# Shorter fixed ends of the first layer's MLP, and second-attention queries made turned in the first layer

## The chip, the cores and the metric

The kernel runs on one core of one Trainium2 chip. The metric is the device time of one execution in microseconds (us). A core has a matrix engine (PE in the profile; its weight loads stand apart as PEld), a vector engine (DVE), a scalar engine (ACT), a third elementwise engine (POOL), a queue engine that starts transfers (SP), and 16 DMA engines. PE multiplies a stationary operand of 128x128 with a moving one (at most 512 columns here) and adds into a PSUM bank (tiles of 128x512 fp32). The kernel uses two rings of four such banks, named `acc` and `misc`.

## The reference

Two layers over 256 tokens of width 1024, in fp32. Each layer is

```python
h = rms_norm(x, attn_norm[l])
p = h @ w_in[l]      # c_q, c_kv, k_rope | mq, mk, mv | rq, rk, rv, rg | three gates
o_mla  = causal attention, 8 heads; q and k, v come from normed c_q (256) and c_kv (128)
o_moba = causal attention, 8 heads of 64: softmax(rope(mq) rope(mk)^T) mv   # one block of 256 holds all tokens
o_ret  = retention, 4 heads, then group norm and silu(rg)
merged = sum over the three of sigmoid(gate) * (o @ w_branch)
x = x + merged @ w_out[l]
h = rms_norm(x, mlp_norm[l])
x = x + square(relu(h @ w_mlp_up[l])) @ w_mlp_down[l]        # 1024 -> 4096 -> 1024
```

and a last `rms_norm` ends it. "Second attention" is `o_moba`; its queries are `mq`, its keys `mk`, its values `mv`. The names `b0` and `c0` stand for the product that holds c_q, c_kv and k_rope (416 columns).

## The kernel before

**Products in three parts.** Every fp32 operand is split into a high part of type fp32r and a low part, the remainder, of the same type. ACT writes the high part (`whi`, L202, for a weight tile; L238 for an activation), DVE the low part (`wlo`, L204; L239). A product is then high by high, high by low and low by high (`three`, L222 to L225). A weight tile is 128x1024: 512 KB, one transfer from SP (L187), one split on ACT and one on DVE. Seven raw tiles and six split ones are held at a time. `load_w` fetches tiles in the order of `weight_plan`, one tile ahead of the one in use. What runs ahead on ACT and DVE is decided by the tile scheduler, which orders the instructions of each engine when the kernel is built, by a simulated clock; `tc.manual_schedule` and `tc.keep_in_program_order` fix the order of what stands in them.

**Two ways round.** `project` keeps tokens on the output's partitions: activations are stationary, weights move. `project_turned` (L371) makes the transposed product: 128 weight columns are stationary, and the high and low halves of the activations move side by side (512 columns, L380), then the low weights with the high half (256 columns, L382). The two halves of the result are joined by an ACT copy (L386) and a DVE add (L387), "the join", and the bank is free after that.

**The program of a layer** is a list `prog` of units (one weight tile or a few), with steps hung on units by `at(slot(unit, j), step)`. Layer 0 begins with eight `start` units, one for each 128 rows of `x`: each multiplies b0 (two `misc` banks) and mq (two `acc` banks, tokens on partitions). When the last is done, `moba_done` copies mq out on ACT (L682) and applies the rotary embedding on DVE; `c_norms` (L648) copies b0 out on ACT (L657), squares it (L660, L661), and norms it; later `moba_turn` (L854) transposes mq on PE, four 128x128 transposes for each half (L860). Layer 1 makes mq by `project_turned` and applies the rotary embedding by `moba_rope` on POOL (`rope_turned` with four small transfers from SP and three POOL operations for each half). In both layers mk is turned: four units `mk 0` to `mk 3` follow, each in one `acc` bank.

**The MLP** walks 32 tiles `f` of the width 4096. `up` makes two of them (L1075: 512 columns; L1077: 256), `squared_relu` splits the result, and `down` (L1091) adds each tile into four quarters of the output (two token halves by two column halves, one `acc` bank each). The last `ENDS = 4` tiles are kept back: their `down` runs quarter by quarter, 12 matmuls each. The last tile (`WHOLE = 1`) is made by `project_t`, with the three parts of 256 columns in one half bank. At the end of layer 0 each quarter, once complete, is copied by ACT (`copied`, L1148), transposed by PE (`turned`, L1154), added to `x` by DVE (L1156), and split for the next layer's norm (`take_part`: four L238 on ACT, four L239 on DVE). The next layer's b0 begins with token half 0 and goes on with half 1; `before(i)` runs the last quarter's `turned(3)` ahead of b0's third unit. The squares of `x` (L271, L274) are summed by POOL (L275) and give the norm's statistics (L295).

Of the kernel before, what the change touches and what calls it, by code (L numbers as in the profile page):

```python
# [18 lines left out]
L = 2  # L19
# [3 lines left out]
ENDS = 4  # L23
# [27 lines left out]
def weight_plan():  # L51
# [14 lines left out]
    for l in range(L):  # L66
# [36 lines left out]
        for f in range(0, NF + 2, 2):  # L103
            for i in (f, f + 1) if f < NF else ():
                block((l, "up", i), "w_mlp_up", KD, span(P * i, P), KD)
            for i in (f - 2, f - 1) if 2 <= f <= NF - ENDS else ():
                plan.append(((l, "down", i, 0), "w_mlp_down", (i, 1), range(D)))
        for i in range(NF - ENDS, NF):
            plan.append(((l, "down", i, 0), "w_mlp_down", (i, 1), range(D)))
# [12 lines left out]
K_COS_MB = K_SIN_MLA + NT * 16  # L122
K_SIN_MB = K_COS_MB + NT * 8

K_TURNED_MLA = K_SIN_MB + NT * 8
# [13 lines left out]
def trunk(ctx: ExitStack, tc: tile.TileContext, gx, wts, consts, gfin, gn, xtok, out):  # L139
# [96 lines left out]
    def split(src, hi, lo, scale):  # L236

        nc.scalar.activation(hi, src, AF.Copy, scale=scale)  # L238
        nc.vector.scalar_tensor_tensor(lo, src, scale, hi.bitcast(F32), op0=ALU.mult, op1=ALU.subtract)  # L239

    def split_plain(src, hi, lo):
        nc.scalar.activation(hi, src, AF.Copy)
        nc.vector.tensor_sub(lo, src, hi.bitcast(F32))
# [4 lines left out]
    class Normed:  # L248
# [28 lines left out]
        def take_part(self, t, half):  # L277

            sl = slice(P * t, P * t + P)
            for n in range(4 * half, 4 * half + 4):  # L280
                hi, lo = self.k(n)
                split(chunk(n)[:, sl], hi[:, sl], lo[:, sl], gain(self.g0 + n))
# [87 lines left out]

    def project_turned(l, key, xn, done):  # L371


        pair = []

        def unit(n):
# [6 lines left out]
            if n % 2 == 0:  # L383
                pair.append(w2k("qkraw"))
            second = sb.tile([P, S], F32, name="second", tag="relu", bufs=3)
            nc.scalar.copy(second, acc[:, S : 2 * S])  # L386
            nc.vector.tensor_add(halves(pair[-1])[:, n % 2, :], acc[:, 0:S], second)  # L387
            if n % 2:
                done(n // 2, pair[-1])
# [251 lines left out]
    def layer(l, xn, before):  # L641
# [6 lines left out]
        def c_norms():  # L648
            accs = b0
            if l:  # L650
                for n in range(KD):
                    xn.square(n)
                xn.stats()
            for t in range(NT):
                ct = w2k("c0")
                c0.append(ct)
                nc.scalar.activation(ct[:, :416], accs[t][:, :416], AF.Copy, scale=xn.col[t])  # L657
                m = small("ssc")
                junk = sb.tile([P, S], F32, name="junk", tag="xsq", bufs=2)
                nc.scalar.activation(junk, ct[:, 0:MLA_QR], AF.Square, accum_out=m[:, 0:1])  # L660
                nc.scalar.activation(junk[:, :MLA_KVR], ct[:, MLA_QR : MLA_QR + MLA_KVR], AF.Square, accum_out=m[:, 1:2])  # L661
                nc.vector.tensor_scalar(m[:, 2:3], m[:, 0:1], 1.0 / MLA_QR, EPS, op0=ALU.mult, op1=ALU.add)
                nc.vector.tensor_scalar(m[:, 3:4], m[:, 1:2], 1.0 / MLA_KVR, EPS, op0=ALU.mult, op1=ALU.add)
                nc.gpsimd.tensor_tensor(m[:, 4:6], m[:, 2:4], neghalf[:, 0:2], op=ALU.pow)
                nc.vector.tensor_scalar(ct[:, 0:MLA_QR], ct[:, 0:MLA_QR], m[:, 4:5], None, op0=ALU.mult)
                kv = ct[:, MLA_QR : MLA_QR + MLA_KVR]
                nc.vector.tensor_scalar(kv, kv, m[:, 5:6], None, op0=ALU.mult)
                kr = ct[:, 384:416].rearrange("p (h two n) -> p h two n", h=1, two=2)
                rope(kr, K_COS_MLA, K_SIN_MLA, t, 16, 1)
                for i in range(2):  # L670
                    dst = krx[t][:, 64 * (1 - i) : 64 * (1 - i) + 64].rearrange("p (two n) -> p two n", two=2)
                    nc.vector.tensor_copy(dst[:, :, 16 * i : 16 * i + 16], kr[:, 0, :, :])

# [4 lines left out]
        def moba_done(key):  # L678
            def done(accs):
                dst = mqkv[key] = [w2k(key) for _ in range(NT)]  # L680
                for t in range(NT):
                    nc.scalar.activation(dst[t], accs[t], AF.Copy, scale=xn.col[t])  # L682
                    if key == "mq":
                        xv = dst[t].rearrange("p (h two r) -> p h two r", h=MB_H, two=2)[:, :, :, 0:8]
                        rope(xv, K_COS_MB, K_SIN_MB, t, 8, MB_H)
# [3 lines left out]
        def start(k, mq):  # L689

            if k == 0:
                b0.extend(misc_tile("b0") for _ in range(NT))
                mq.extend(acc_tile() for _ in range(NT))
            before(k)
            ah, al = xn.k(k)
            if k == 0:

                blocks = [(mq, slice(0, 256), load_w(l, "mq", 0), 0, True), (mq, slice(256, 512), load_w(l, "mq", 1), 0, False)]
                blocks.append((b0, slice(0, 416), load_w(l, "b0", 0), 0, True))
            else:  # L700
                w = load_w(l, "b0mq", k)
                blocks = [(b0, slice(0, 416), w, 0, False), (mq, slice(0, 512), w, 416, False)]

            for part in ("high", "low"):
                for accs, cs, w, c, begins in blocks:
                    ws = slice(c, c + cs.stop - cs.start)
                    for t in range(NT):
                        o, sl = accs[t][:, cs], slice(P * t, P * t + P)
                        if part == "high":
                            nc.tensor.matmul(o, ah[:, sl], w[0][:, 0, ws], start=begins, stop=False)  # L710
                            nc.tensor.matmul(o, al[:, sl], w[0][:, 0, ws], start=False, stop=False)  # L711
                        else:
                            nc.tensor.matmul(o, ah[:, sl], w[1][:, 0, ws], start=False, stop=k == KD - 1)  # L713
            if k == KD - 1:
                moba_done("mq")(mq)
# [14 lines left out]
        if l:  # L730
            project_turned(l, "mq", xn, moba_pair("mq"))
            at(slot("mq", 1), c_norms)
            at(slot("mq", 2), xn.stats_row)
        else:
# [3 lines left out]
            at(slot("start", KD - 2), lambda: xn.stats_rows(xrows))  # L738
            at(slot("start", KD - 1), c_norms)
# [6 lines left out]
        def c_turn():  # L746
# [5 lines left out]
            for k in range(3):  # L752
                pt = pts[k // 2][:, (k % 2) * S : (k % 2) * S + S]
                for t in range(NT):
                    nc.tensor.transpose(pt[:, P * t : P * t + P], c0[t][:, P * k : P * k + P], ident)
# [98 lines left out]
        def moba_turn(i):  # L854

            pt = misc_tile("pq")
            for a in range(2):
                for t in range(NT):
                    k = 2 * i + a
                    nc.tensor.transpose(  # L860
                        pt[:, (2 * a + t) * P : (2 * a + t + 1) * P], mqkv["mq"][t][:, P * k : P * k + P], ident
                    )
            o = sb.tile([P, 2 * S], F32, name="qkT", bufs=4)
            nc.scalar.copy(o, pt)
            qkT["mq"][i] = halves(o)

# [137 lines left out]
        at(slot("rg", 0), lambda: in_a_row(ret_scores, moba_last))  # L1004
# [55 lines left out]
        def up(fs, between=None):  # L1060
# [4 lines left out]
            if fs[0] >= NF - WHOLE:  # L1065
# [14 lines left out]
        def squared_relu(f, u):  # L1080
            s = sb.tile([P, S], F32, name="relu", bufs=3)
            if f < NF - WHOLE:
                nc.scalar.copy(s, u[:, S : 2 * S])
                nc.vector.tensor_add(s, u[:, 0:S], s)
            nc.vector.scalar_tensor_tensor(s, s if f < NF - WHOLE else u[:, 0:S], 0.0, xm.row, op0=ALU.max, op1=ALU.mult)  # L1085
            nc.scalar.activation(s, s, AF.Square)  # L1086
            both = sb.tile([P, 2, S], F32R, name="sq", tag="w2k", bufs=W2K)
            split_plain(s, both[:, 0, :], both[:, 1, :])
# [26 lines left out]
        h2 = {}  # L1115
# [192 lines left out]
```

## Time and profile before

| | |
|---|---|
| median of 3 runs | 836.45 us (836.05 to 836.94) |
| the profiled execution, its own time | 836.87 us |
| its span in the trace | 835.1 us |
| busy: PE, PEld, DVE, ACT, POOL | 827.2, 702.9, 585.2, 482.1, 92.5 us |
| HBM read, written | 151.00 MB, 1.05 MB |

A row of a timeline gives start, length, engine, line, operation, tiles and shape; "x4" joins four in a row, and the bracket tells how long the engine had idled before it and what released it. Matmuls overlap in the pipeline (a 512-column one lasts 0.39 us, and the next starts 0.23 us later), so costs of PE are taken from start to start, or from the chain of work that ended last, which lists each piece by what it added.

### The profile page before, as it was taken

The numbers are of one execution on the slowest core, as the hardware profiler recorded it, in microseconds if no ns is written. First come the engines' busy times: TensorE is split into PE (matmuls) and PEld (weight loads), VectorE is DVE, ScalarE is ACT, GpSimd is POOL, SyncE is SP. The second block draws the span as 40 slices with busy tenths as digits, with TensorE's granted clock in tenths as the row PEclk, the third lists the DMA queues.
The fourth block names the chain that finished last, engine by engine and source line by source line (L and its number), as shares of the span: only waits on it lengthen the run. The fifth ranks groups of instructions, "written<-read, shape, count | busy, mean of one in ns | idle before, by whom it ended". The sixth has DMA issues, their size and how long they took to land.

```text
span 835.1 us, 12150 instructions
## 1 busy us (share of the span) xinstructions
PE 827.2 (99%) x4374; PEld 702.9 (84%) x4374; DVE 585.2 (70%) x1057; ACT 482.1 (58%) x858; POOL 92.5 (11%) x82
## 2 busy tenths in 40 slices
PE   9999999999999999999999999999999999999997
PEld 7888878888888888888889888888888888888886
DVE  6878567595787666666599876766868776556663
ACT  7766665445556555555676575664545555555552
POOL 0221000040030000000038111002201200000000
PEclk9999999999999999999999999999999999999999
DMA  9956644646456566565466657545565656666611
GB/s 349 362 177 212 228 141 146 195 133 219 140 187 225 183 199 186 193 193 167 131 227 194 204 178 236 157 142 188 156 199 161 219 171 192 198 196 187 197 53 50
DMA packets 45708, 155.98 MB, mean 187 GB/s; under 512 B 5712, under 2 KB 6736, under 8 KB 45392
## 3 DMA queue, kind: packets, MB, share of 16 engines
q1 hardware_dynamic: 45072, 154.54, 58.4%
q8 instruction: 34, 0.56, 0.3%
q10 hardware_dynamic: 576, 0.67, 0.2%
q14 instruction: 26, 0.21, 0.1%
HBM read 151.00 MB, written 1.05 MB: 182 GB/s over the span
## 4 chain that ended last, share of the span: by engine, by line
PE 98%; DVE 1%; ACT 0%; issue 0%; DVEq 0%
PE acc L223 18%; PE acc L225 18%; PE acc L224 18%; PE pup L1075 14%; PE pup L1077 7%; PE acc L1025 5%; PE acc L380 4%; PE acc L382 2%; PE ps_pt L483 1%; PE ps_s L835 1%; PE po L510 1%; PE ps_s L449 1%; DVE wlo L204 1%; PE acc L710 1%; PE acc L711 1%; PE acc L713 0%
## 5 line engine op out<-in xcount | busy, mean ns | idle before, releaser
L204 DVE TENSOR_TENSOR wlo<-raw,whi 128x1024 fp32r<-128x1024 f32 (+4 forms) x287 | 346.7, 1216 | 181.5 <-ACT whi L202 128.1
L202 ACT ACTIVATE whi<-raw 128x1024 fp32r<-128x1024 f32 (+4 forms) x287 | 292.0, 1023 | 188.4 <-PE acc L225 105.6
L1075 PE MATMUL pup<-xs,whi 128*128 128x512 f32 x496 | 121.5, 390 | 0.0
L225 PE MATMUL acc<-whi,xs 128*128 128x512 f32 (+1 forms) x304 | 119.3, 393 | 0.4 <-DVE xs L239 0.4
L223 PE MATMUL acc<-whi,xs 128*128 128x512 f32 (+1 forms) x304 | 119.6, 395 | 0.0
L224 PE MATMUL acc<-wlo,xs 128*128 128x512 f32 (+1 forms) x304 | 118.9, 391 | 0.0
L1075 PEld LDWEIGHTS pup<-xs,whi 128*128 128x128 f32 x496 | 91.9, 188 | 18.3
L223 PE MATMUL acc<-whi,sq 128*128 128x512 f32 x256 | 100.1, 391 | 0.0
L224 PE MATMUL acc<-wlo,sq 128*128 128x512 f32 x256 | 99.9, 390 | 0.0
L225 PE MATMUL acc<-whi,sq 128*128 128x512 f32 x256 | 98.8, 389 | 0.0
L1077 PE MATMUL pup<-xs,wlo 128*128 128x256 f32 x496 | 68.8, 283 | 0.0
L1077 PEld LDWEIGHTS pup<-xs,wlo 128*128 128x128 f32 x496 | 65.7, 191 | 3.1
L225 PEld LDWEIGHTS acc<-whi,xs 128*128 128x128 f32 x304 | 57.1, 188 | 12.3 <-DVE xs L239 0.7
L223 PEld LDWEIGHTS acc<-whi,xs 128*128 128x128 f32 x304 | 57.1, 188 | 11.7 <-issue 0.8
L224 PEld LDWEIGHTS acc<-wlo,xs 128*128 128x128 f32 x304 | 57.2, 188 | 10.5
L1086 ACT ACTIVATE relu<-relu 128x256 f32<-128x256 f32 x64 | 25.5, 408 | 54.4 <-DVE relu L1085 54.4
L225 PEld LDWEIGHTS acc<-whi,sq 128*128 128x128 f32 x256 | 48.1, 188 | 10.2
L223 PEld LDWEIGHTS acc<-whi,sq 128*128 128x128 f32 x256 | 48.2, 188 | 9.2
L224 PEld LDWEIGHTS acc<-wlo,sq 128*128 128x128 f32 x256 | 48.2, 188 | 8.9
L275 POOL TENSOR_TENSOR sqsum<-sqsum,xsq 128x256 f32<-128x256 f32 x21 | 23.3, 1111 | 290.8 <-issue 172.4
L472 ACT ACTIVATE prob<-prob,smx 128x128 f32<-128x128 f32 x64 | 28.4, 445 | 24.9 <-DVE smx L469 24.9
L380 PE MATMUL acc<-xs,whi 128*128 128x512 f32 x160 | 41.3, 395 | 0.7 <-DVE qkraw L387 0.7
(239 smaller groups left out, 1147.6 us busy)
## 6 DMA issues: line engine op xcount, KB each, us to landing
raw<-wts SPq DMA_DIRECT2D x264, 512.0 KB, 4.2
raw<-wts SPq DMA_DIRECT2D x6, 464.0 KB, 7.8
qkoth<-qkraw SPq DMA_DIRECT2D x40, 64.0 KB, 4.3
dec<-consts SPq DMA_DIRECT2D x2, 1024.0 KB, 5.0
raw<-wts SPq DMA_DIRECT2D x4, 416.0 KB, 3.2
xrow<-xtok SPq DMA_DIRECT2D x4, 256.0 KB, 8.0
gn<-gn SPq DMA_DIRECT2D x2, 512.0 KB, 5.5
raw<-wts SPq DMA_DIRECT2D x3, 256.0 KB, 4.1
```

The lines of the kernel that those rows point to most:

```text
L202: nc.scalar.activation(hi[:, cs], raw[:, cs], AF.Copy)
L204: nc.vector.tensor_sub(lo[:, cs], raw[:, cs], hi[:, cs].bitcast(F32))
L223: nc.tensor.matmul(o, ah, bh, start=start, stop=False)
L224: nc.tensor.matmul(o, ah, bl, start=False, stop=False)
L225: nc.tensor.matmul(o, al, bh, start=False, stop=stop)
L275: (nc.gpsimd if n < self.on_pool else nc.vector).tensor_add(self.sum, self.sum, sq)
L380: nc.tensor.matmul(acc, wh[:, k, :], xn.both(k), start=k == 0, stop=False)
L472: nc.scalar.activation(p[:, a:b], p[:, a:b], AF.Exp, bias=m[:, 2 + i : 3 + i], scale=scale, accum_out=m[:, 4 + i : 5 + i])
L1025: nc.tensor.matmul(o, a, b, start=half == 0 and i == 0, stop=4 * half + n == KD and i == len(jobs) - 1)
L1075: nc.tensor.matmul(u, w, xm.both(k), start=k == 0, stop=False)
L1077: nc.tensor.matmul(u[:, 0:S], w, xm.k(k)[0], start=False, stop=k == KD - 1)
L1086: nc.scalar.activation(s, s, AF.Square)
```

## The change

- `ENDS` and `WHOLE` become lists by layer. Layer 0 keeps back two tiles instead of four, and its last tile is made in a pair like the others; layer 1 stays as it was. In layer 0 the four quarters end in plain order, six matmuls each.
- At the end of layer 0, four of the next layer's weight tiles (b0 0 to 3) are fetched ahead of the quarters (`have`). `behind` names instructions that a tile's splits are scheduled behind: b0 2 and 3 behind the split of the last MLP tile, mq 0 behind the last quarter's splits. The first quarter's copy and add keep their place in the program.
- Layer 0's mq is made turned inside the `start` units, in four `acc` banks, and joined in the last unit; the weights of mk 1 and mk 2 are split behind the joins. `moba_turn`, the old rotary embedding of mq and its tables in `consts` go; `moba_rope` runs for mq in layer 0 too, at `gmla1`.
- b0 is copied and squared without the norm's factor (`c_copies`), which is applied afterwards (`c_norms`); in layer 1 the squares of `x` move from mq 1 to b0's last unit, with two of the eight sums on DVE, and the copies to mq 0.
- The retention scores move from slot `rg` 0 to `rg` 1 in both layers.

```diff
-ENDS = 4
+ENDS, WHOLE = [2] * (L - 1) + [4], [0] * (L - 1) + [1]
...
     def load_w(*key):
         ahead = 0 if key[:2] in ((0, "b0"), (0, "mq"), (0, "b0mq")) else AHEAD
-        while order and len(loaded) < ahead + 1:
+        have(min(ahead + 1, len(loaded) + len(order)))
+        return loaded.pop(key)
+    behind = {}
+    def have(n):
+        while len(loaded) < n:
             first = order.pop(0)
-            loaded[first] = fetch(first)
-        return loaded.pop(key)
+            with ExitStack() as pinned:
+                for ins in behind.get(first, ()):
+                    pinned.enter_context(tc.issue_after(ins.ins))
+                loaded[first] = fetch(first)
...
+    def joins(done):
+        pair = []
+        def join(n, acc):
+            if n % 2 == 0:
+                pair.append(w2k("qkraw"))
+            second = sb.tile([P, S], F32, name="second", tag="relu", bufs=3)
+            both = nc.scalar.copy(second, acc[:, S : 2 * S]), nc.vector.tensor_add(
+                halves(pair[-1])[:, n % 2, :], acc[:, 0:S], second
+            )
+            if n % 2:
+                done(n // 2, pair[-1])
+            return both
+        return join
...
-        def c_norms():
-            accs = b0
-            if l:
-                for n in range(KD):
-                    xn.square(n)
-                xn.stats()
+        def c_copies():
             for t in range(NT):
                 ct = w2k("c0")
-                nc.scalar.activation(ct[:, :416], accs[t][:, :416], AF.Copy, scale=xn.col[t])
...
+                nc.scalar.activation(ct[:, :416], b0[t][:, :416], AF.Copy)
...
-                mq.extend(acc_tile() for _ in range(NT))
+                mq.extend(acc_tile() for _ in range(4))
...
+            def turned_part(part, ns):
+                for n in ns:
+                    if part == 0:
+                        nc.tensor.matmul(mq[n], wq[n][0], xn.both(k), start=k == 0, stop=False)
+                    else:
+                        nc.tensor.matmul(mq[n][:, 0:S], wq[n][1], ah, start=False, stop=k == KD - 1)
...
+            if k < KD - 1:
+                for part in range(2):
+                    for job in (turned_part, b0_part) if k == 0 else (b0_part, turned_part):
+                        job(part, range(4)) if job is turned_part else job(part)
+            else:
+                join = joins(moba_pair("mq"))
+                for part in range(2):
+                    turned_part(part, [0])
+                for part in range(2):
+                    b0_part(part)
+                for n in range(1, 4):
+                    for part in range(2):
+                        turned_part(part, [n])
+                have(1)
+                for n in range(4):
+                    behind[l, "mk", 1, 0] = behind[l, "mk", 2, 0] = join(n, mq[n])
...
         if l:
             project_turned(l, "mq", xn, moba_pair("mq"))
+            for n in range(KD):
+                at(slot("b0", 7), lambda n=n: xn.square(n))
+            at(slot("mq", 0), c_copies)
             at(slot("mq", 1), c_norms)
...
+            at(slot("start", KD - 1), c_copies)
             at(slot("start", KD - 1), c_norms)
...
-            if l:
-                at(slot("mk", 1 + 2 * i), lambda i=i: moba_rope("mq", i))
+            at(slot("mk", 1 + 2 * i) if l else slot("gmla1", 2 * i), lambda i=i: moba_rope("mq", i))
...
-        if l == 0:
-            for i in range(2):
-                at(first + 4 * i - 3, lambda i=i: moba_turn(i))
...
-        at(slot("rg", 0), lambda: in_a_row(ret_scores, moba_last))
+        at(slot("rg", 1), lambda: in_a_row(ret_scores, moba_last))
...
-                us = up([f, f + 1]) if f + 2 < NF else up([f]) + up([f + 1])
+                us = up([f, f + 1]) if f + 1 < NF - WHOLE[l] else up([f]) + up([f + 1])
...
+        ends = [lambda q=q: finish(q, range(ENDS[l])) for q in range(4)]
+        if last:
+            ends[0] = lambda: (finish(0, range(3)), finish(1, range(2)), finish(0, range(3, 4)))
+            ends[1] = lambda: finish(1, range(2, 4))
         if not last:
-            xn = Normed(G_ATT + KD * (l + 1), KD)
+            xn = Normed(G_ATT + KD * (l + 1), KD - 2)
             ys = {}
+            have(ENDS[l])
+            for j in range(ENDS[l], 4):
+                behind[l + 1, "b0", j] = latest
+            have(4)
...
             def before(i):
                 if i == 2:
-                    turned(3)
+                    behind[l + 1, "mq", 0, 0] = turned(3)
```

More of the change, by code (lines that the diff above doesn't have):

```diff
@@ L382, in unit @@
                 nc.tensor.matmul(acc[:, 0:S], wl[:, k, :], xn.k(k)[0], start=False, stop=k == KD - 1)
[L383 to L389, printed above, removed]
+            join(n, acc)
         for n in range(4):
@@ L704, in start @@
[L704 to L713, printed above, removed]
@@ L1129, in layer @@
                     down(w, h2[g], *q, g)
-        ws = [load_w(l, "down", f, 0) for f in range(NF - ENDS, NF)]
+        ws = [load_w(l, "down", f, 0) for f in range(first_end, NF)]
         order_pe = ExitStack()
@@ L1220 @@
 FIRST = 4
-WHOLE = 1
 AHEAD = 1
```

120 lines of the change are left out of this document (61 added, 59 removed).

## The prediction

> **What bounds the kernel now.** I read the page first: its busy shares and its chain of waits.
>
> ```profile
> PE 827.2 (99%) x4374; PEld 702.9 (84%) x4374; DVE 585.2 (70%) x1057; ACT 482.1 (58%) x858; POOL 92.5 (11%) x82
> PE 98%; DVE 1%; ACT 0%; issue 0%; DVEq 0%
> ```
>
> PE works from end to end, and the chain that ended last is PE for 98%. So an edit counts only if it takes matmul time away or closes a hole in PE. The other engines matter where they are late. The second view was the waits of PE; beside the start of the program it has two rows.
>
> ```profile
> PE acc L380 <- DVE qkraw L387: 0.7, 1, 0.7
> PE acc L225 <- DVE xs L239: 0.4, 1, 0.4
> ```
>
> Both lie at the border of the layers, which is where the change fixes an order. The timeline of PE shows both from start to start.
>
> ```profile
> 421.41 0.34 PE L224 MATMUL acc<-wlo,xs 128*128 128x416 f32 x1
> 422.15 0.46 PE L225 MATMUL acc<-whi,xs 128*128 128x416 f32 x1 [0.39 <-DVE xs L239]
> ...
> 433.21 0.97 PE L380 MATMUL acc<-xs,whi 128*128 128x512 f32 x3 [0.70 <-DVE qkraw L387]
> ```
>
> Without the wait the matmul at 422.15 would have begun 0.19 us after the one at 421.41 (a 416-column matmul is 416/512 of 0.23, below), so at 421.60: 0.55 lost. At 433.21 the bracket gives the hole, 0.70. Together 1.25 us is all that order can win there.
>
> **The change part by part.**
>
> *Transposes removed.* Layer 0's `moba_turn` goes: two groups of four on PE.
>
> ```profile
> 113.40 0.39 PE L225 MATMUL acc<-whi,omlal 128*128 128x512 f32 x1
> 113.63 0.60 PE L860 MATMUL pq<-K,mq 128*128 128x128 f32 x4
> 113.99 0.48 PE L223 MATMUL acc<-whi,omlah 128*128 128x512 f32 x1
> 114.30 0.40 PE L224 MATMUL acc<-wlo,omlah 128*128 128x512 f32 x1
> ```
>
> Between the matmuls at 113.40 and 114.30 there would be two steps of 0.23 (113.63 - 113.40), 0.46, and there are 0.90: 0.44 for a group, 0.88 for both. The rest of `moba_turn`, two ACT copies, lies beside PE and is worth nothing.
>
> *The last MLP tile of layer 0 made in a pair.* The chain gives the pieces (start, what it added).
>
> ```profile
> 387.44 3.63 PE pup L1075 x16
> 391.07 1.91 PE pup L1077 x16
> ...
> 398.45 1.81 PE pup L1075 x8
> ...
> 404.10 0.23 PE acc L223
> ```
>
> A pair costs 3.63 + 1.91 = 5.54; the last two tiles, made apart, 404.10 - 398.45 = 5.65. Gain 0.11.
>
> *mq made turned.* For each of eight row blocks the old form has six matmuls of 512 columns, the new one four of 512 and four of 256. By the pair above, 512 columns take 3.63 / 16 = 0.23 and 256 take 1.91 / 16 = 0.12: 6 x 0.23 = 1.38 against 4 x 0.23 + 4 x 0.12 = 1.40. That is level, and I count nothing. The start is not level: the first matmul now needs both halves of the activations.
>
> ```profile
> 4.21 0.58 PE L710 MATMUL acc<-whi,xs 128*128 128x256 f32 x1
> 4.59 0.49 PE L711 MATMUL acc<-whi,xs 128*128 128x256 f32 x1
> 4.88 0.41 PE L710 MATMUL acc<-whi,xs 128*128 128x256 f32 x1
> ```
>
> And the low half on DVE:
>
> ```profile
> 3.96 0.48 DVE L266 SCALAR_TENSOR_TENSOR xs<-GX,xs 128x256 fp32r<-128x256 f32 x1
> ```
>
> The low half is ready at 4.44 and the matmul that reads it began at 4.59; the new first one begins there too, 0.38 after the old. In that 0.38 one 256-column matmul ran; the next took 0.29 (4.88 - 4.59), where 0.12 is usual: the start is slow. Bounds 0.12 (what the work is worth later) and 0.38 (all of the delay); I take 0.2, nearer to the row of usual pace, since the delayed work comes when the slow rows are nearly over. The Trainium skill ("TensorE: Matmul & The Clock Gate", Part 1) says the slow phase is a budget of time, about 3.4 us, and not of matmuls. By that the delay costs half of itself, 0.19, and by a count of matmuls all of it, 0.38; the trace cannot tell them apart here.
>
> *From the start to mk.* All four `acc` banks now hold mq, and mk 1 and 2 are split behind the joins, where splits used to run ahead. The chain's first mk unit:
>
> ```profile
> 26.02 1.84 PE acc L380 x8
> 27.86 0.95 PE acc L382 x8
> ```
>
> The groups of ACT between 26 and 37 us (busy, mean ns of one):
>
> ```profile
> L202 ACT ACTIVATE whi<-raw 128x1024 fp32r<-128x1024 f32 (+1 forms) x7 | 7.0, 1014 | 0.9 <-PE acc L380 0.7 <-PE acc L713 0.2
> L386 ACT COPY second<-acc 128x256 f32<-128x256 f32 x3 | 1.2, 396 | 0.0
> L657 ACT ACTIVATE c<-b,ms 128x416 f32<-128x416 f32 x2 | 1.1, 613 | 0.0
> L660 ACT ACTIVATE junk<-c 128x256 f32<-128x256 f32 x2 | 0.9, 436 | 0.0
> L661 ACT ACTIVATE junk<-c 128x128 f32<-128x128 f32 x2 | 0.7, 340 | 0.0
> ```
>
> The last mq bank is complete at about 26.0. Its join's copy (0.4) and mk 1's high split (1.0) put mk 1 at 27.4 to 27.6, and PE wants it at 26.02 + 1.84 + 0.95 = 28.8: slack 1.2. Behind the wait stand mk 2, mk 3 and the copies of b0 on ACT. Those copies and squares are 1.1 + 0.9 + 0.7 = 2.7, and four join copies 1.6. b0 is complete three mq blocks early (3 x 0.35 = 1.05), so at about 25.0; if all 4.3 go first, mk 1's split ends at 25.2 + 4.3 + 1.0 = 30.5, and PE waits 1.7. Bounds 0 and 1.7. I take 0, since the joins are all that must come first, and 1.2 us of the copies may go before without harm. If that cover is gone it is the first rival.
>
> *Two tiles at the end, splits in order.* At the border, a quarter's copy on ACT:
>
> ```profile
> 409.60 0.58 ACT L1148 COPY ydn<-acc 128x512 f32<-128x512 f32 x1 [0.78 <-PE acc L225]
> ```
>
> The rows of DVE, and the sums on POOL:
>
> ```profile
> 410.04 0.69 DVE L1156 TENSOR_TENSOR GX<-GX,pyd 128x512 f32<-128x512 f32 x1 [3.73 <-PE pyd L1154]
> 411.20 1.23 DVE L239 SCALAR_TENSOR_TENSOR xs<-GX,xs 128x128 fp32r<-128x128 f32 x4 [0.47 <-ACT xs L238]
> 414.87 1.02 DVE L204 TENSOR_TENSOR wlo<-raw,whi 128x832 fp32r<-128x832 f32 x1 [0.93 <-ACT whi L202]
> 417.46 2.15 DVE L204 TENSOR_TENSOR wlo<-raw,whi 128x832 fp32r<-128x832 f32 x2
> 420.13 1.22 DVE L204 TENSOR_TENSOR wlo<-raw,whi 128x1024 fp32r<-128x1024 f32 x1
> 421.27 2.65 DVE L239 SCALAR_TENSOR_TENSOR xs<-GX,xs 128x128 fp32r<-128x128 f32 x4
> 425.98 6.84 DVE L204 TENSOR_TENSOR wlo<-raw,whi 128x1024 fp32r<-128x1024 f32 x5
> 432.75 0.41 DVE L387 TENSOR_TENSOR qkraw<-acc,second 128x256 f32<-128x256 f32 x1
> 421.10 3.49 POOL L275 TENSOR_TENSOR sqsum<-sqsum,xsq 128x256 f32<-128x256 f32 x4 [172.37 <-issue]
> ```
>
> The matmul count does not change: 24 go from the four quarters to before them. From the first quarter's add (410.04) to the matmul that should have begun at 421.60 DVE had 11.56 us, and was 0.55 late. 12 matmuls fewer stand between the two now, 12 x 0.23 = 2.76, so 8.8 us are left, and with the same work DVE would be 0.55 + 2.76 = 3.3 late. What leaves that stretch is the weight splits, 1.02 + 2.15 + 1.22 = 4.4: two b0 tiles ahead of the quarters, where DVE idled 3.73 (and the 24 moved matmuls give 5.5 more), and mq 0 and what follows it behind the last quarter. POOL's sums go later too, in whose company four xs splits took 2.65 instead of 1.23. So the 0.55 is gone, with about 1.1 of reserve (4.4 - 3.3). For each quarter PE has 6 x 0.23 = 1.38 to cover the ACT copy (0.58), which leaves 0.8 for the ways there and back. The second hole: at 432.75 the join stood behind five splits in a row, 6.84 us. In the new order two of these ran earlier, and the bank need not be mq's, since b0's banks are copied out without waiting for the statistics. I count 0.70 as won. What is late next is nothing that I see; bounds for both holes together are 0 and 1.25 won, and I take 1.25, as the moved work exceeds the lateness.
>
> *The rest.* The retention scores one unit later meet no wait of PE in the list above: nothing won. The values that need them now come two units of 12 matmuls later instead of three, 5.5 us (24 x 0.23), enough for four DVE products of the size of a join (0.41 each) and the splits between them; I count nothing lost. Layer 0's mq ropes add eight small transfers on SP and six POOL operations; below.
>
> The sum: -0.88 - 0.11 + 0.2 - 1.25 = -2.04 us. The profiled execution took 836.87, 0.42 over the median of 836.45: 836.87 - 2.04 = 834.83 for its like, and 836.45 - 2.04 = 834.4 against the median, 0.24% faster. The measurement of this kernel can tell about 0.2%, 1.67 us, from no change; the limit is 834.78.
>
> **The rivals.** *Start wait.* mk 1's split stands behind all of b0's copies: +1.7, sum -0.3, 836.1. For it: ACT and the chain of waits are densest there, and nothing fixes b0's copies behind mk 1. Against: 1.2 us of slack.
>
> *Order without effect.* The holes stay as they are, because each is one engine's queue being late by half a microsecond and any reordering can make another. Then the sum is -2.04 + 1.25 = -0.8, 835.7. This is also the case that the change does not do what it says.
>
> *Short quarters (slower).* If the b0 tiles' splits do not run ahead of the quarters (their raw tiles or split buffers come free too late), the stretch keeps its 4.4 us of splits in 8.8 us. DVE is then 3.3 late where it was 0.55, and the second hole stays as well: -0.88 - 0.11 + 0.2 + 2.76 = +2.0, 838.4. It decides from the point where less than 3.3 of the 4.4 leaves. For it: a split buffer comes free only when a `down` has used its tile. Against: the two `down` tiles moved ahead are used up before the quarters begin.
>
> *POOL in DVE's way (slower).* The four splits that took 2.65 beside POOL instead of 1.23 show the price. The window of the first gate stage (length, then busy and count of PE, PEld, DVE, ACT, POOL):
>
> ```profile
> 62.00:84.00 22.00, 22.00 (x111) 18.53 (x110) 19.50 (x53) 14.42 (x34) 3.02 (x3) 1.00 0.65 207
> ```
>
> Six operations of 512 columns, twice the 3.49 / 4 = 0.87 of a 256-column one each, are 10.5 us of POOL. If DVE stands still for half of that and all falls into this window, where it has 2.5 idle, it is 2.7 late: -2.04 + 2.7 = +0.7. From 7 us of standing still (4.5 late) the case is slower by the measure above: +2.5, 838.9. Against: layer 1 already makes the same six operations beside DVE, and the waits of PE have no row for it. The Trainium skill ("SBUF — State Buffer", Who interferes with whom) speaks against this change here: DVE and GpSimd (POOL) share one port pair, a lock held for the whole instruction. The 2.65 beside 1.23 agrees.
>
> **How the numbers follow.** Forecast, 834.4: 0.60; inside it runs from 833.5 to 835.3 by the bounds of the start and the holes and a few tenths of rescheduling, and 0.13 of the 0.60 lies in its part above 834.78. Start wait 0.13, order without effect 0.16, short quarters 0.08, POOL 0.03. Faster by over 0.2%: 0.60 - 0.13 = 0.47; within: 0.13 + 0.13 + 0.16 = 0.42; slower: 0.11. The range 833.3 to 837.2 takes in the two middle cases with a us above them, and leaves out the two slower ones and 0.05 below.
>
> **What would show it.** Right: PE has no L380 or L225 wait near 410 to 425 us; the group `pq` is gone; the first real matmul begins at about 4.6; the first mk unit follows the last mq block without a hole. Wrong: a PE wait on ACT `whi` at 28 us (start wait), on DVE `xs` at the border of the layers, of 1 us and more (short quarters), or on `wlo` between 75 and 100 us (POOL); or the holes move to another line while PE's busy time falls by 1 us.

## The result, and the profile after

The changed kernel takes 840.39 us (839.27 to 841.25, 5 runs), the one before 836.45 (836.05 to 836.94, 5 runs beside it): ratio 1.0046 (95% interval 1.0035 to 1.0058). That is 3.9 us slower where 2.0 us faster was forecast, and above the range. The profiled execution of the changed kernel is one of 840.39, with a span of 838.6.

On the page PE is busy for 99% of the span, as it was. The chain that ended last tells more: PE's share of it falls from 98% to 94%, and ACT, DMA and more of DVE stand in it.

```profile
PE 828.0 (99%) x4368; PEld 701.4 (84%) x4368; DVE 591.7 (71%) x1058; ACT 482.0 (57%) x859; POOL 98.6 (12%) x86
PE 94%; DVE 2%; DMA 1%; ACT 1%; issue 1%; POOL 0%; SPq 0%; DVEq 0%; POOLq 0%
```

PE's waits (us in total, times, longest):

```profile
PE acc L233 <- DVE wlo L213: 1.7, 1, 1.7
...
PE acc L232 <- ACT mv L709: 0.7, 1, 0.7
PE acc L232 <- ACT Q L832: 0.7, 1, 0.7
PE acc L732 <- DVE xs L276: 0.3, 1, 0.3
PE acc L232 <- DVE qkraw L390: 0.3, 1, 0.3
PE pct L807 <- DVE c L699: 0.2, 1, 0.2
```

The two rows of the border are gone. `xs` at L732 is the forecast delay at the start, and `qkraw` at L390 lies in the second layer. The other four are new and lie in the first layer, between 46 and 60 us, as PE's timeline shows:

```profile
46.90 0.33 PE L807 MATMUL pct<-K,c 128*128 128x128 f32 x1 [0.21 <-DVE c L699]
...
49.13 0.50 PE L233 MATMUL acc<-wlo,xs 128*128 128x512 f32 x1 [1.68 <-DVE wlo L213]
...
58.03 0.39 PE L232 MATMUL acc<-cTh,whi 128*128 128x256 f32 x1 [0.66 <-ACT Q L832]
...
59.71 0.39 PE L232 MATMUL acc<-cTh,whi 128*128 128x256 f32 x1 [0.71 <-ACT mv L709]
```

To place all of it, I took every step from one matmul's start to the next and subtracted the usual one for its width (0.227 us for 512 columns, 0.187 for 416, 0.119 for 256, 0.112 for 128). The rest, by stretch, in us; "c part" is the second layer's, from its mq to its values. The last five columns are kernels of the next section.

| stretch | before | after | e1 | e5 | e9 | e10 | e12 |
|---|---|---|---|---|---|---|---|
| start to first mk unit | 3.03 | 3.06 | 2.26 | 2.37 | 3.17 | 2.37 | 3.12 |
| mk to first scores, layer 1 | 0.35 | **4.70** | 2.98 | 2.10 | 0.31 | 0.29 | 0.28 |
| first scores to MLP | 0.24 | 0.49 | 0.23 | 0.18 | 0.30 | 0.27 | 0.27 |
| border of the layers | 2.01 | **0.68** | 0.68 | 0.68 | 0.68 | 0.69 | 1.56 |
| c part, layer 2 | 0.12 | 0.68 | 0.85 | 0.99 | 0.40 | 0.14 | 0.15 |
| from there to MLP, layer 2 | 0.37 | 0.90 | 1.21 | 0.67 | 0.46 | 0.46 | 0.46 |

Added up, the rows are 4.39 more after than before, and the usual steps 0.88 less; that makes 3.5, as the two spans do (838.6 and 835.1). The border gave about what was forecast (-1.33), and one stretch, from mk to the first scores, lost 4.35. Another 1.3 went in smaller holes: 0.25 ahead of the first MLP, 0.56 and 0.53 in the second layer. What comes late in the stretch that lost most is the normed c. ACT, before and after:

```profile
30.41 0.44 ACT L660 ACTIVATE junk<-c 128x256 f32<-128x256 f32 x1
...
33.66 0.33 ACT L661 ACTIVATE junk<-c 128x128 f32<-128x128 f32 x1
```

```profile
28.27 3.49 ACT L211 ACTIVATE whi<-raw 128x1024 fp32r<-128x1024 f32 x4
31.64 0.43 ACT L680 ACTIVATE junk<-c 128x256 f32<-128x256 f32 x1
...
36.11 0.32 ACT L680 ACTIVATE junk<-c 128x128 f32<-128x128 f32 x1
```

The squares of c now come behind four weight splits that had waited for the joins, and the last one starts 2.45 us later. The powers on POOL, which make the norm factors of c out of the sums of squares, follow; first before, then after:

```profile
34.13 2.45 POOL L664 TENSOR_TENSOR ssc<-ssc,neghalf 128x2 f32<-128x2 f32 x2 [13.37 <-DVE ssc L663]
36.56 2.42 POOL L399 TENSOR_TENSOR tab<-TAB,rrow 128x256 f32<-128x256 f32 x2
```

```profile
40.12 1.44 POOL L421 TENSOR_TENSOR tab<-TAB,rrow 128x256 f32<-128x256 f32 x2 [19.17 <-DMA TAB<-consts]
41.52 0.71 POOL L690 TENSOR_TENSOR ssc<-ssc,neghalf 128x2 f32<-128x2 f32 x1
42.19 1.31 POOL L437 TENSOR_TENSOR qkT<-qkraw,tab 128x512 f32<-128x512 f32 x1
43.46 0.75 POOL L690 TENSOR_TENSOR ssc<-ssc,neghalf 128x2 f32<-128x2 f32 x1
44.18 3.81 POOL L437 TENSOR_TENSOR qkT<-qkraw,tab 128x512 f32<-128x512 f32 x3
```

With the sums late, the scheduler wrote the order of POOL with the tables ahead of the powers (in e9 below, where the sums are early, the powers go first), and the tables wait for a transfer. On SP that transfer stands behind weight loads, which wait for raw tiles that the late splits hold; first before, then after:

```profile
28.92 0.42 SPq L826 DMA_DIRECT2D TAB<-consts  x1
```

```profile
33.12 0.42 SPq L878 DMA_DIRECT2D TAB<-consts  x1
```

The last sum is there at 38.5, the first power starts at 41.52. And POOL has four cosine products now (the first of the three POOL operations of each rotary embedding), between and behind the powers: mk's two, which it had before, and mq's two. DVE pays for both:

```profile
38.30 0.23 DVE L689 TENSOR_SCALAR ssc<-ssc,s 128x2 f32<-128x2 f32 x1
...
42.26 1.65 DVE L699 TENSOR_SCALAR c<-c,ssc,ms 128x256 f32<-128x256 f32 x2 [1.94 <-POOL ssc L690]
44.24 2.61 DVE L699 TENSOR_SCALAR c<-c,ssc,ms 128x256 f32<-128x256 f32 x2 [0.33 <-POOL ssc L690]
46.77 4.58 DVE L213 TENSOR_TENSOR wlo<-raw,whi 128x1024 fp32r<-128x1024 f32 x3
```

Behind the products of c stand three weight splits, and for the first of them PE waits 1.7 us.

### The profile page after: what moved, and what is told of

Its sections match the earlier page's. It is cut to its first block, busy times and chain, and to the rows that moved or that the text cites. A ratio compares the mean times of both kernels' runs of the same rounds, so it can differ in the third digit from the quotient of the medians.

```text
span 838.6 us, 12159 instructions
## 1 busy us (share of the span) xinstructions
PE 828.0 (99%) x4368; PEld 701.4 (84%) x4368; DVE 591.7 (71%) x1058; ACT 482.0 (57%) x859; POOL 98.6 (12%) x86
## 4 chain that ended last, share of the span: by engine, by line
PE 94%; DVE 2%; DMA 1%; ACT 1%; issue 1%; POOL 0%; SPq 0%; DVEq 0%; POOLq 0%
PE acc L232 18%; PE acc L233 18%; PE acc L234 17%; PE pup L1110 14%; PE pup L1112 7%; PE acc L1060 5%; PE acc L408 3%; PE acc L410 1%; PE ps_pt L505 1%; PE ps_s L886 1%; PE acc L732 1%; PE po L532 1%; DVE wlo L213 1%; DMA TAB<-consts 1%; PE ps_s L471 1%
## 5 line engine op out<-in xcount | busy, mean ns | idle before, releaser
L1110 PE MATMUL pup<-xs,whi 128*128 128x512 f32 x504 | 123.3, 390 | 0.0
```

Source lines behind the costliest of these rows:

```text
L1110: nc.tensor.matmul(u, w, xm.both(k), start=k == 0, stop=False)
```

## The experiments

All theories take c's late norm as the place and differ in what makes it late or dear. A: POOL's order and the late table, behind which the powers wait. B: ACT and DVE are late by themselves, ahead of POOL. C: POOL's cosine products slow down DVE's splits. From e5 on, D: PE's own order sets the stretch; from e9 on, E: the squares behind the held splits start it all. G is on the border: its holes are handed on to the next wait.

Every kernel but e4, e6 and e8 is the changed one with the edit shown; times are medians, ratios go against the kernel before, run beside it.

**e1, the powers first on POOL.**

```diff
-                    mqkv["tab"] = tables(xn, TAB)
+                    with ExitStack() as pinned:
+                        for ins in pows if l == 0 else ():
+                            pinned.enter_context(tc.issue_after(ins.ins))
+                        mqkv["tab"] = tables(xn, TAB)
```

> The changed kernel with one order fixed on POOL: the two powers that give the norm factors of c_q and c_kv in layer 0 are issued ahead of the table products, which wait for the TAB transfer. Theory A (POOL queue: the powers stood behind tables that waited 19 us for TAB, the normed c came about 7 us late, and PE stood still where it is transposed): the four first-layer holes between 46 and 60 us, 3.9 us, go; 840.4 - 3.9 = 836.5 or less. Theory B (DVE is late on its own account, because the weight splits now come behind the joins): the powers are earlier but the holes stay within 1 us, 839.5 to 841. Theory C (POOL's rope products hold up DVE, the c products took 1.65 and 2.61 us for two): holes stay, as the rope products stay; 839 to 841.

Measured: 838.29 us, 1.0015 (1.0007 to 1.0024).

**e2, the table loaded at the start.**

```diff
     nc.sync.dma_start(K, consts[:, :K_DEC])
+    nc.sync.dma_start(TAB, consts[:, K_TURNED_MB:])
...
-            at(slot("mv", 3), lambda: tc.keep_in_program_order(nc.sync.dma_start(TAB, consts[:, K_TURNED_MB:])))
```

> The changed kernel with the TAB transfer moved to the start of the program, behind that of K. Theory A: no wait for TAB on POOL, whatever its order; the holes between 46 and 60 us go, 836 to 837; the 256 KB ahead of the mk weights may cost up to 0.7 us if PE waits for them. Theory B and C: 839.5 to 841.

Measured: 838.52 us, 1.0021 (1.0013 to 1.003). e1 and e2 each give back some 2 us, and the stretch from mk to the first scores falls from 4.70 to 2.98 and 3.59. So the queue of POOL behind its transfer is a part of the loss; it isn't all of it. e2 takes the wait for the table away, but not the powers' late place, for a cosine product now stands ahead of them:

```profile
38.33 2.41 POOL L437 TENSOR_TENSOR qkT<-qkraw,tab 128x512 f32<-128x512 f32 x1 [8.41 <-DVE ssc L690]
40.71 2.43 POOL L691 TENSOR_TENSOR ssc<-ssc,neghalf 128x2 f32<-128x2 f32 x2
```

In e1, where the powers start at 36.55, DVE still had this:

```profile
39.44 3.11 DVE L699 TENSOR_SCALAR c<-c,ssc,ms 128x256 f32<-128x256 f32 x4
42.47 6.79 DVE L213 TENSOR_TENSOR wlo<-raw,whi 128x1024 fp32r<-128x1024 f32 x3
49.18 0.86 DVE L249 SCALAR_TENSOR_TENSOR cTl<-pct,GX,cTh 128x256 fp32r<-128x256 f32 x2
```

while POOL ran the cosine products:

```profile
41.11 7.06 POOL L437 TENSOR_TENSOR qkT<-qkraw,tab 128x512 f32<-128x512 f32 x4
```

**e3, the splits of mk 1 and mk 2 not held behind the joins.**

```diff
-                    behind[l, "mk", 1, 0] = behind[l, "mk", 2, 0] = join(n, mq[n])
+                    join(n, mq[n])
```

> The changed kernel without the rule that the weights of mk 1 and mk 2 are split behind the joins of mq. Raw tiles come free earlier, and POOL has the powers ahead of the tables again. Theory A: TAB is issued up to 4 us earlier, the holes between 46 and 60 us go, 836.5 or less, unless a wait of mk 0 for its bank (a join behind two splits, up to 2 us) takes their place. Theory C: the rope products are as before, 839 to 841.

Measured: 840.5 us, 1.0046 (1.0032 to 1.006).

```profile
27.73 1.45 PE L408 MATMUL acc<-xs,whi 128*128 128x512 f32 x5 [2.00 <-DVE qkraw L390]
```

The first mk unit waits 2.0 us for a bank, and what is won behind it (the stretch falls from 4.70 to 2.86) is lost here. So simply dropping the holding back is no cure; its price is what gets pushed behind the splits that it holds.

**e4, the border part alone, on the kernel before.**

```diff
-ENDS = 4
+ENDS, WHOLE = [2] * (L - 1) + [4], [0] * (L - 1) + [1]
...
+            have(ENDS[l])
+            for j in range(ENDS[l], 4):
+                behind[l + 1, "b0", j] = latest
+            have(4)
...
+                if q == 0:
+                    tc.keep_in_program_order(copy)
...
-                    turned(3)
+                    behind[l + 1, "mq", 0, 0] = turned(3)
```

> The kernel before with the border of the layers alone changed: two tiles at the end of layer 0, plain order of the quarters, the pair at the end, b0 tiles split ahead; start, norms and retention slot as before. Both holes at the border (1.25) and 0.11 go by the prediction: 836.45 - 1.36 = 835.1. If the changed norm statistics of layer 1 are what emptied the second hole, 0.7 stays: 835.8. No effect: 836.4.

Measured: 836.62 us, 1.0002 (0.9994 to 1.0011): nothing. The first hole is gone, and the time is waited out behind it (the last three rows of the table come to 2.5, as in the kernel before):

```profile
431.55 0.61 PE L306 MATMUL pss<-ones,sqsum 128*128 128x1 f32 x4 [0.36 <-POOL sqsum L285]
432.97 2.11 PE L391 MATMUL acc<-xs,whi 128*128 128x512 f32 x8 [0.81 <-DVE qkraw L398]
```

**e5, e1 and the cosine products held until KK (the keys of the first attention) is written.** A one-column POOL copy reads KK; the products are put behind it.

```diff
+                    gate.append(nc.gpsimd.tensor_copy(small("gate")[64:P, 0:1], KK[64:P, 0, 0:1]))
...
+            for ins in after:
+                pinned.enter_context(tc.issue_after(ins.ins))
             engine.tensor_mul(halves(o), halves(raw), cos)
```

> The changed kernel with the two powers of the first layer ahead of the tables on POOL (as in e1) and one small POOL copy that reads KK put ahead of the four cosine products, so that POOL starts these only when VectorE has written the splits of c and KK. Theory C (POOL's rope products beside VectorE's splits are what is left of the first layer's loss: three splits took 6.79 us in e1 where three take 3.67 alone, so 3.1 us of VectorE's time): splits of weights near 42 to 46 us fall back to 1.2 us each, the cTl splits start near 46 instead of 49.2, the hole of TensorE before the first attention scores falls from 2.98 us over nominal to under 1.5, time 836.6 to 837.2. Rival D (TensorE's own order of the steps after the turn of c, with their banks waiting for ScalarE's copies of Q and mv, sets the stretch): VectorE runs earlier but the excess stays over 2.5 us, time 838.0 to 838.5. If the products held back become late themselves, a wait for qkT appears ahead of the second attention's scores.

Measured: 836.71 us, 1.0001 (0.9991 to 1.001). The splits beside which POOL is idle take 1.22 to 1.29 each again:

```profile
41.88 2.58 DVE L213 TENSOR_TENSOR wlo<-raw,whi 128x1024 fp32r<-128x1024 f32 x2 [0.22 <-ACT whi L211]
45.96 1.22 DVE L213 TENSOR_TENSOR wlo<-raw,whi 128x1024 fp32r<-128x1024 f32 x1 [1.50 <-ACT whi L211]
47.10 0.87 DVE L249 SCALAR_TENSOR_TENSOR cTl<-pct,GX,cTh 128x256 fp32r<-128x256 f32 x2
```

So theory C, the rope products in DVE's way, accounts for a second part. The time is 1.6 us under e1; in the stretch itself the trace shows 0.9 of it (2.98 to 2.10), between what C and D had forecast, and 0.4 lies in the second layer, which the edit doesn't touch. The stretch still has 2.10, mostly the two waits on ACT's copies of Q and mv. In the table the first stretch is left out of such comparisons: with equal work there it comes out anywhere from 2.24 to 3.17, and the steps that differ lie between 4 and 7 us.

**e6, the kernel before with the border part and the second layer's new norm statistics; e8, the same with the new statistics in the first layer too** (mq as before in both; the last three lines are e8's alone).

```diff
+            for n in range(KD):
+                at(slot("b0", 7), lambda n=n: xn.square(n))
+            at(slot("mq", 0), c_copies)
-            at(slot("mq", 1), c_norms)
+            at(slot("mq", 1), c_norms_new)
...
-            at(slot("start", KD - 1), c_norms)
+            at(slot("start", KD - 1), c_copies)
+            at(slot("start", KD - 1), c_norms_new)
```

> The kernel before with the border part of the change and the second layer's new norm statistics (squares a step earlier, copies of c unscaled at the first mq unit), and its old first layer. If the border holes are closed by these two together: both waits (VectorE xs, VectorE qkraw) gone, the border's excess near 0.7 instead of 2.05, time 836.45 - 1.3 - 0.1 = 835.0 (834.7 to 835.5). Rival: the emptied holes come back in the second layer's c part (0.12 to 0.68 us there in the changed kernel): 835.6. If the border needed the changed first layer for another reason, it stays at 836.6.

> e6 with the new norm statistics in the first layer too, whose mq is still made in rows and rotated on VectorE, so that POOL has no cosine product of mq there and SP no late load of the table. If the loss of the first layer comes from the turned mq and what it puts on POOL and SP: same as e6 within 0.3 us. If the new form of the norm statistics itself is late there (products with two factors, copies of c ahead): up to 2 us above e6.

Measured: e6 836.53 us, 0.9999 (0.999 to 1.0008); e8 836.39, 1.0002 (0.9993 to 1.0011). In e6 the hole at the bank is closed, 0.4 is left at the sums on POOL, and this comes new:

```profile
456.62 0.39 PE L232 MATMUL acc<-cTh,whi 128*128 128x256 f32 x1 [0.42 <-DVE qkraw L398]
```

e8, whose first layer has the new statistics without the turned mq, loses nothing: the new form of the sums is not what is late.

**e7, the changed kernel without the border part**, e4's edit taken back:

```diff
-ENDS, WHOLE = [2] * (L - 1) + [4], [0] * (L - 1) + [1]
+ENDS, WHOLE = [4] * L, [1] * L
...
-                    behind[l + 1, "mq", 0, 0] = turned(3)
+                    turned(3)
```

> The changed kernel with four tiles at both MLP ends and without the fixed order of the splits at the border; its first layer and norm statistics stay. If the two parts add: 840.39 + 0.55 + 0.11 (first hole and the pair) = 841.0, and with the second hole too 841.7. If the border is worth nothing without the norm statistics and the other way round, 841.7; if the norm statistics alone close the second hole, 841.0.

Measured: 840.7 us, 1.0048 (1.0036 to 1.0061), 0.3 above the changed kernel. Both by itself and inside the slow kernel the border part is worth next to nothing; here the last three rows of the table come to 2.2, against 2.26 in the changed kernel.

**e9, the squares of c ahead of the held splits.** Nothing else is edited, POOL's order least of all.

```diff
-                    nc.scalar.activation(junk[:, :n], ct[:, cs], AF.Square, ...)
+                    sqs.append(nc.scalar.activation(junk[:, :n], ct[:, cs], AF.Square, ...))
+            if l == 0:
+                behind[l, "mk", 2, 0] = [*behind[l, "mk", 2, 0], *sqs]
```

> The changed kernel with one thing more: the second unit of mk's splits after the first held (mk 2) is put behind the four squares of c on ScalarE, which in the changed kernel come behind four weight splits (first done at 30.94, last at 35.6 us in e5; 30.41 to 33.9 before). No edit to POOL's queue. Theory E (the splits piled up behind the joins push the squares of c, with them the sums, the powers and the products of c, and all that POOL and TensorE have behind them): squares done near 30, products of c near 33 to 36 as before or earlier, the excess between the first mk unit and the first scores falls from 4.70 to under 1.5, time 836.5 to 837.3 (what POOL's cosine products cost VectorE may stay: up to 3 us of its time, hidden if the turn of c comes before them). Rival C again (the cosine products beside the splits, whatever their time): 838 or more. Rival F: VectorE now waits for the powers ahead of mk 2's split, and TensorE stands before the third mk unit: 838 to 840 with a wait on wlo near 33 us.

Measured: 835.2 us, 0.9983 (0.9974 to 0.9992): 5.2 us under the changed kernel from the place of four ACT instructions. In the trace 4.4 of it is the stretch from mk to the first scores; 0.7 lies in the second layer, which the edit doesn't touch. ACT:

```profile
27.32 0.92 ACT L676 ACTIVATE c<-b 128x416 f32<-128x416 f32 x2
28.12 0.40 ACT L334 ACTIVATE rrow<-pss 128x256 f32<-128x256 f32 x1
28.38 0.44 ACT L681 ACTIVATE junk<-c 128x256 f32<-128x256 f32 x1
...
29.73 0.34 ACT L681 ACTIVATE junk<-c 128x128 f32<-128x128 f32 x1
...
30.03 5.38 ACT L211 ACTIVATE whi<-raw 128x1024 fp32r<-128x1024 f32 x6
```

The powers go first on POOL by themselves, and the table is still late, at no cost:

```profile
29.94 1.57 POOL L696 TENSOR_TENSOR ssc<-ssc,neghalf 128x2 f32<-128x2 f32 x2 [8.29 <-DVE ssc L695]
41.55 1.44 POOL L421 TENSOR_TENSOR tab<-TAB,rrow 128x256 f32<-128x256 f32 x2 [10.04 <-DMA TAB<-consts]
42.95 6.48 POOL L437 TENSOR_TENSOR qkT<-qkraw,tab 128x512 f32<-128x512 f32 x4
```

DVE has multiplied c by 33.3 us, and what POOL slows down now is work with room:

```profile
32.66 0.66 DVE L705 TENSOR_SCALAR c<-c,ssc,ms 128x256 f32<-128x256 f32 x2
...
44.23 2.35 DVE L213 TENSOR_TENSOR wlo<-raw,whi 128x1024 fp32r<-128x1024 f32 x1 [1.32 <-ACT whi L211]
46.51 1.78 DVE L822 COPY KK<-krT 64x1024 f32<-64x1024 f32 x1
48.30 1.70 DVE L823 COPY KK<-krT 64x1024 f32<-64x1024 f32 x1
```

Beside the start, PE has one wait left, the forecast delay of its first matmul, and no other:

```profile
PE acc L738 <- DVE xs L276: 0.4, 1, 0.4
```

**e10, e5 and e9 together**, the edits as shown there.

> e5 (powers first, the cosine products held until KK is written) and the squares of c ahead of mk 2's splits. In e5 two holes of 0.81 and 0.87 us were left, in which TensorE waits at a bank that ScalarE has still to copy (Q, mv), and c came 2.5 us later than before. If those holes are the rest of the late c (theory E): both gone, excess between the first mk unit and the first scores near 0.4, time 836.71 - 1.7 = 835.0. If they come from the order of TensorE alone: they stay, 836.5. If VectorE waits for the powers in front of mk 2's split: a hole near 33 us, 837 to 838.

Measured: 834.76 us, 0.998 (0.9972 to 0.9989). It is the fastest of all, and both kernels are beaten; its interval overlaps that of e9, so what the holding of the products adds once c is early isn't settled.

**e11, the retention scores back at their old place.**

```diff
-        at(slot("rg", 1), lambda: in_a_row(ret_scores, moba_last))
+        at(slot("rg", 0), lambda: in_a_row(ret_scores, moba_last))
```

> The changed kernel with the first retention scores back at their old place, at the first unit of the retention gate instead of the second. The prediction had it at nothing: 840.4 within 0.4. In the traces the stretch from the first scores to the MLP is 0.25 us over before: if it is this slot, 840.1 in the first layer and as much again in the second, 839.9.

Measured: 838.75 us, 1.0032 (1.0019 to 1.0045), lower than either expectation. **e13** is the same edit on e10:

> e10 with the first retention scores at their old place. e11 came out 1.64 us under the changed kernel, of which its trace gives 0.75 to the first 7 us and 0.54 to a hole in the second layer's c part that e10 does not have. If the slot itself costs something, 834.0 or less; if e11's gain was the start and that hole, 834.5 to 835.0.

Measured: 835.58 us, 0.999 (0.9982 to 0.9999), 0.8 above e10, with this wait in the second layer:

```profile
PE ps_s L903 <- DVE KK L848: 0.4, 1, 0.4
```

The edit has no steady price: it went down by 1.6 on one kernel and up by 0.8 on the other, and each time small holes in the second layer's c part or scores came or went. Both intervals overlap those of their bases; the slot's own worth stays open.

**e12, e10 without the border part**, by e7's edit.

> e10 without the border part of the change (four tiles at both MLP ends, no fixed order of the splits there); first layer and norm statistics stay as in e10. The prediction's border term: +0.55 for the first hole and +0.11 for the pair, the second hole closed by the norm statistics: 834.76 + 0.66 = 835.4; by its whole border term 834.76 + 1.36 = 836.1. Theory G (holes at the border are handed on, since the joins and sums behind them set when the second layer's c part can run; e4 and e6 gained nothing from the border, e7 lost 0.3): within 0.3 of e10, 834.8 to 835.1, with the first hole back and a smaller one behind it.

Measured: 835.61 us, 0.9987 (0.9978 to 0.9996), 0.85 above e10 (the two intervals overlap; the trace has 0.87 in this stretch). Both holes are back, the second smaller and now behind ACT's copy of c:

```profile
421.43 0.45 PE L234 MATMUL acc<-whi,xs 128*128 128x416 f32 x1 [0.39 <-DVE xs L249]
...
432.02 2.11 PE L408 MATMUL acc<-xs,whi 128*128 128x512 f32 x8 [0.26 <-ACT c L679]
```

So by e10 and e12 the border part gives about 0.9 in a kernel whose other queues are on time, and in e4, e6 and e7 it was handed on to the next wait. That isn't settled, though. The last three rows of the table together also move where no edit touches the second layer (2.74 in e1, 2.26 in the changed kernel, 1.54 in e9, 1.29 in e10), and e13, which has the border part, comes to 2.5 by the same measure, more than e12 without it (2.17).

## Why the prediction was wrong

**The step that failed is "From the start to mk".** It saw the conflict (the held splits against b0's copies and squares on ACT, 2.7 us of them) and asked one question of it: does mk 1's split come late for PE? It doesn't: its high split ends at 27.3, where 27.4 to 27.6 was forecast, and PE goes on to mk without a hole. The other side, what the copies and squares of c have behind them when the splits go first, was not priced: the term was 0, its upper bound 1.7, and the stretch behind it lost 4.35. It is a chain of five steps on four engines: squares on ACT, sums on DVE, powers on POOL, products on DVE, turn on PE. e9 shows it: putting the four squares first, alone, takes the stretch from 4.70 to 0.31 and the time from 840.39 to 835.2. The powers' place behind the table (e1: 1.7 of the stretch) and POOL beside DVE (e5: 0.9 more) are how the late squares cost so much; neither costs anything clear of the noise once the squares are early (e9, e10).

**"The rest" and its place.** The POOL operations of mq's rope were costed in the window from 62 to 84 us, by the place of their step in the program. Their cosine products run from 42 us, with mk's, as soon as their operands are there, beside the splits that the c part needs. What they do to DVE was of the size that the rival *POOL in DVE's way* had (three splits 6.79 for 3.67 alone); its window was wrong, so that its own sign, a wait on `wlo` between 75 and 100 us, came at 47. None of the rivals was the cause by its own terms; *short quarters*, with its wait on `xs` at the border, did not occur.

**Transposes, pair, mq level.** The group `pq` is gone, and the matmuls' usual steps sum to 0.88 less, where the forecast had 0.99: 0.90 for the eight transposes and 0.09 for the pair are won, and 0.11 is lost on mq. The prediction had called mq level from 1.40 against 1.38 for one row block, and there are eight of them. Once the holes are away (e10), the last matmul starts 2.80 us earlier than before: 0.88 of usual steps, 1.32 of the border, 0.66 of the start, nothing else over 0.1. The part of the start lies within the spread that the next paragraph names, and is luck. By the medians e10 gains 1.70, where the sum said 2.04.

**Start, +0.2.** The first real matmul starts at 4.66 (forecast 4.6), and the first mk unit at 25.92 for 25.78, +0.14. That agrees, but shows little: the same stretch differs by 0.9 between profiled executions.

**Border, -1.25 for the holes.** In the trace it is right (2.01 to 0.68), and both waits are gone. As a term to be added it was over-sized: alone the border part gave nothing that can be measured (e4), nor did it with the second layer's new statistics (e6); in the mended kernel it gave 0.85 together with the tile pair, as far as e10 and e12 can tell, where 1.36 was forecast. In the changed kernel 1.1 of the 1.33 is lost again between the second layer's mq and its MLP. "What is late next is nothing that I see" was the weak sentence: next were POOL's sums (0.36 in e4), and the join before the c part (0.42 in e6, 0.29 in the changed kernel). That the second hole closes through the earlier statistics, as the step said of b0's banks, e4 and e6 bear out.

**Retention slot, 0.** Open, as told at e13.

## What to carry to other kernels

When a change holds one engine's work behind another's, price both sides: whether the held work is in time, and what everything that it now stands in front of sets off on the other queues. Four instructions of 0.4 us that begin a chain over four engines belong ahead of splits of 1.0 us that have slack, and where a scheduler writes the order from a simulated clock, their place may have to be pinned. A hole closed on the bounding engine is a gain only after the next wait has been looked up, so take a gain at a border as won only when the queues behind it are on time too.

## What the runs showed of the hardware

POOL and DVE slow each other down. In e1 three splits of 128x1024 took 6.79 us beside POOL, 2.26 each, against 1.22; the four products on POOL took 7.06 in the same time, 1.77 each, against 1.29 for one beside little DVE work. DVE so lost 3.1 us beside 7.1 us of POOL, not far from the half that the prediction had allowed; that POOL is slowed too, it had not. Together they took nearly as long as one after the other would have (3 x 1.22 + 4 x 1.29 = 8.8 us of work between 41.1 and 49.2, 8.1 us, in which DVE also ended the products of c). The Trainium skill ("SBUF — State Buffer", Who interferes with whom) has the port pair that the two share as an exclusive lock; this row comes near to that, but a lock that is never shared would have taken at least the 8.8. Who pays differs: in the changed kernel three products took 3.81 on POOL, 1.27 each, while two products of c on DVE took 2.61 where e9 has 0.66.

The same two powers of 128x2 elements took 2.45 us before, 3.34 in e1 and 1.57 in e9. In e1 two weight splits on DVE ran beside them, before one, in e9 none; whether that makes the difference was not tested.
